# Last inverse roots moved off GpSimd, and shorter final waits, at the end of an eight-core encoder layer

## Chip, cores, metric

One Trainium2 chip, all 8 cores, one launch; each core works on its own two prompt streams (8192 rows) and 32 sample rows. The metric is the device time in microseconds (us) of the slowest core. Executions fall into states: in a *slow* one, one die or both are granted a lower TensorE clock and the time is some per cent longer, whatever the kernel.

Engine names in profile lines: PE is TensorE (PEld its weight loads), DVE VectorE, ACT ScalarE, POOL GpSimd, SP SyncE. A `q` behind a name (SPq) means that the sequencer did it: a wait, a DMA issue, a drain. A semaphore is a counter that a finished instruction or a landed DMA raises and that others wait for; a drain is an instruction at which an engine finishes what it has begun before it goes on.

## The reference, cut to what matters

```python
x = x + rms_norm(merged @ w_out, n_post_mix)
h2 = rms_norm(x, n_pre_ffn)
g, up = jnp.split(h2 @ w_ffn_in, 2, axis=-1)
x = x + rms_norm((jax.nn.silu(g) * up) @ w_ffn_out, n_post_ffn)      # the last step of a tile
# rms_norm(x, g): x * rsqrt(mean(x * x) + 1e-6) * g, in float32
```

The kernel takes 16 tiles of 512 rows, one after the other.

## The kernel before

A small recording layer keeps a list of instructions for each engine and works out the waits. At the end it emits the lists inside a block; the block closes with a drain on each engine and a barrier. SyncE alone waits for all DMA semaphores of the program.

```python
def run(eng_name, e, final=False):
    for o in self.ops[eng_name]:
        ...                                   # the op's own waits, the op, its semaphore (cut)
    if final:                                 # SyncE only
        for k in self.dma_keys:               # 91 semaphores
            e.wait_ge(dsem[k], self.dma_count[k])
```

An inverse root is made of two GpSimd operations on 128x1, multiply-add and power:

```python
def rsqrt(P, c, eps, scale=1.0 / D, eng=POOL):
    o, i_ = stt[0:P, c + 1:c + 2], stt[0:P, c:c + 1]
    ts(eng, o, i_, float(scale), float(eps), ALU.mult, ALU.add, SK(c), SK(c + 1))
    tt(POOL, o, o, negh[0:P, 0:1], ALU.pow, SK(c + 1) + ["negh"], SK(c + 1))   # negh = -0.5
```

In the last tile, row blocks 0 to 2 (128 rows each) go through `PostNorm`: Square with accumulation on ScalarE, `rsqrt`, a multiply and an add on VectorE, a 512 KB store from SyncE. The last row block comes in two halves of 512 columns, so that the first is squared while TensorE makes the second:

```python
def last_rows(n):
    ...
    act(hst[:, n, 0:512], ps[:, b, :], AF.Square, ..., accum_out=stt[:, lc + n:lc + n + 1])
    tt(DVE, lt[:, n, :], ps[:, b, :], gS[:, 3, cs], ALU.mult, ...)
    o = stt[:, lc + 2 + n:lc + 3 + n]
    ts(POOL, o, stt[:, lc + n:lc + n + 1], 1.0 / D, stt[:, lc + 2:lc + 3] if n else EPS, ALU.mult, ALU.add, ...)
    if n == 0:
        return
    tt(POOL, o, o, negh[:, 0:1], ALU.pow, ...)
    for k in range(2):
        sttop(xt[:, 3, cs], lt[:, k, :], o, xt[:, 3, cs], ALU.mult, ALU.add, ...)
        m.dma((SP, ACT)[k], uniq("so"), yp[...], xt[:, 3, cs], ...)          # 256 KB each
```

The softmax here doesn't subtract the row's maximum and nothing guards it: scores larger than these inputs give would overflow.

Of the kernel before, what the change touches and what calls it, by code (L numbers as in the profile page):

```python
# [6 lines left out]
F32 = mybir.dt.float32  # L7
# [9 lines left out]
D = 1024  # L17
# [16 lines left out]
class MK:  # L34
    def __init__(self, nc):
        self.nc = nc
        self.ops = {e: [] for e in ENGS}
        self.last_w = {}
        self.readers = {}
        self.known = {e: [-1] * len(ENGS) for e in ENGS}  # L40
        self.known_dma = {e: {} for e in ENGS}
        self.dma_count = {}
        self.dma_keys = []
        self.pending = {e: [] for e in ENGS}
        self.stage = "setup"

# [23 lines left out]
    def _add(self, eng, emit, reads, writes, dma_sem=None):  # L70
        op = Op(eng, emit)
        op.tag = self.stage
        lst = self.ops[eng]
        op.idx = len(lst)
        deps = self._deps(reads, writes, eng)
        if self.pending[eng]:
            deps.extend(self.pending[eng])
            self.pending[eng] = []
        kn = self.known[eng]
        kd = self.known_dma[eng]  # L80
        best = {}
        for t in deps:
            k = (t[0], t[1])
            o = best.get(k)
            if o is None or t[2] > o[2]:
                best[k] = t
        for t in best.values():
            if t[0] == "e":
                _, de, di, dclk = t
                if de == eng and eng in (PE, SP):  # L90
                    continue
                j = EIDX[de]
                if kn[j] >= di:
                    continue
                if de == eng and eng != POOL and dma_sem is None and op.idx - di >= 4:
                    continue
                op.waits.append(("e", de, di))
                self.ops[de][di].need_inc = True
                kn[j] = di
                for jj, v in enumerate(dclk):  # L100
                    if v > kn[jj]:
                        kn[jj] = v
            else:
                _, sk, val = t
                if kd.get(sk, 0) >= val:
                    continue
                assert val == self.dma_count[sk], ("ambiguous DMA semaphore wait", sk, val, self.dma_count[sk])
                op.waits.append(("d", sk, val))
                kd[sk] = val
        if dma_sem is not None:  # L110
            if dma_sem not in self.dma_count:
                self.dma_count[dma_sem] = 0
                self.dma_keys.append(dma_sem)
            self.dma_count[dma_sem] += 16
            op.dma_sem = dma_sem
            op.dma_val = self.dma_count[dma_sem]
            tok = ("d", dma_sem, op.dma_val)
        else:
            clk = list(kn)
            clk[EIDX[eng]] = op.idx  # L120
            tok = ("e", eng, op.idx, tuple(clk))
        for k in writes:
            self.last_w[k] = tok
            self.readers[k] = []
        for k in reads:
            if k not in writes:
                self.readers.setdefault(k, []).append(tok)
        lst.append(op)
        return op
# [21 lines left out]
    def finish(self):  # L151
        nc = self.nc
        with ExitStack() as st:
            esem = {e: st.enter_context(nc.semaphore("s_" + e)) for e in ENGS}
            dsem = {k: st.enter_context(nc.semaphore("d_%d" % i)) for i, k in enumerate(self.dma_keys)}
            semval = {}
            for e in ENGS:
                c = 0
                vals = []
                for o in self.ops[e]:  # L160
                    if o.need_inc:
                        c += 1
                    vals.append(c)
                semval[e] = vals
            block = st.enter_context(nc.Block())

            def run(eng_name, e, final=False):
                for o in self.ops[eng_name]:
                    for w in o.waits:
                        if w[0] == "e":  # L170
                            e.wait_ge(esem[w[1]], semval[w[1]][w[2]])
                        else:
                            e.wait_ge(dsem[w[1]], w[2])
                    ins = o.emit(e)
                    if o.dma_sem is not None:
                        ins.then_inc(dsem[o.dma_sem], 16)
                    elif o.need_inc:
                        ins.then_inc(esem[eng_name], 1)
                if final:
                    for k in self.dma_keys:  # L180
                        e.wait_ge(dsem[k], self.dma_count[k])

            @block.tensor
            def _(e):
                run(PE, e)

            @block.scalar
            def _(e):
                run(ACT, e)

            @block.vector
            def _(e):
                run(DVE, e)

            @block.gpsimd
            def _(e):
                run(POOL, e)

            @block.sync
            def _(e):  # L200
                run(SP, e, final=True)
# [3 lines left out]
def build_program(n_prompt_tiles=16, do_sample=True):  # L205
# [33 lines left out]
    with ExitStack() as st:  # L239
# [27 lines left out]
        es2 = sb("es2", [128, 8], F32)  # L267
        g0T = sb("g0T", [128, 8], F32)
        negh = sb("negh", [128, 4], F32)
        ident = sb("ident", [128, 128], BF16)  # L270
        ones = sb("ones", [128, 128], BF16)
        WmT = sb("WmT", [128, 4, 128], BF16)
# [31 lines left out]
            m.op(PE, lambda e: e.transpose(out=out, in_=in_, identity=idn), reads=reads + ["ident"],  # L304
                 writes=[("ps", TB)])

        def act(out, in_, func, reads, writes, scale=1.0, accum_out=None):
            kw = {} if accum_out is None else {"accum_out": accum_out}
            m.op(ACT, lambda e: e.activation(out=out, in_=in_, func=func, scale=scale, **kw), reads=reads,  # L309
                 writes=writes)  # L310

# [153 lines left out]
        def rsqrt(P, c, eps, scale=1.0 / D, eng=POOL):  # L465
# [2 lines left out]
            ts(eng, o, i_, float(scale), float(eps), ALU.mult, ALU.add, SK(c), SK(c + 1))  # L468
            tt(POOL, o, o, negh[0:P, 0:1], ALU.pow, SK(c + 1) + ["negh"], SK(c + 1))

        def slot_(P, slot):

            if slot < 2:
                return hst[0:P, slot, :], [("hst", slot)]
            return PT[0:P, slot - 2].rearrange("p h n -> p (h n)"), [("PT", slot - 2)]
# [16 lines left out]
            copy(ACT, dst, pTv[:, 0:8 * P].rearrange("p (k t) -> p k t", k=8), B(TB), dk)  # L492

        class PostNorm:
            def __init__(self, P, pair, gi, x, xk, eps_mul=1.0, dst=None):
                self.P, self.pair, self.gi, self.x, self.xk = P, pair, gi, x, xk
                self.eps, self.dst = EPS * eps_mul, dst

            def square(self, junk=None):
                P, b = self.P, self.pair  # L500
                self.t, self.tk, _ = tmp2()
                self.c = stat(2)
                out, ok = junk or (self.t[0:P], self.tk)
                act(out, ps[0:P, b:b + 2, :], AF.Square, B(b, b + 1), ok + SK(self.c),
                    accum_out=stt[0:P, self.c:self.c + 1])
                rsqrt(P, self.c, self.eps)

            def apply(self):
                P, b = self.P, self.pair
# [36 lines left out]
        m.op(POOL, lambda e: e.memset(negh[:], -0.5), writes=["negh"])  # L546
        act(stt[:, 62:63], negh[:, 0:1], AF.Exp, ["negh"], SK(62))
        m.op(POOL, lambda e: e.memset(ones[:], 1.0), writes=["ones"])
        t0_, t0k = tmp1()
        m.op(POOL, lambda e: e.memset(t0_[:, 0:128], 1.0), writes=t0k)  # L550
        affine(t0_[:, 0:128], [[-1, 128]], ALU.is_equal, 0, 1, t0k[0])
# [863 lines left out]
        def ffn(T, N):  # L1415
# [74 lines left out]
            def last_rows(n):  # L1490
# [2 lines left out]
                b, cs = 6 + n, slice(512 * n, 512 * n + 512)  # L1493
                act(hst[:, n, 0:512], ps[:, b, :], AF.Square, B(b), [("hst", n), *SK(lc + n)],
                    accum_out=stt[:, lc + n:lc + n + 1])
                tt(DVE, lt[:, n, :], ps[:, b, :], gS[:, 3, cs], ALU.mult, B(b) + [("gS", 3)], [ltk[n]])
                o = stt[:, lc + 2 + n:lc + 3 + n]
                ts(POOL, o, stt[:, lc + n:lc + n + 1], 1.0 / D, stt[:, lc + 2:lc + 3] if n else EPS, ALU.mult, ALU.add,
                   SK(lc + n) + (SK(lc + 2) if n else []), SK(lc + 2 + n))
                if n == 0:  # L1500
                    return
                tt(POOL, o, o, negh[:, 0:1], ALU.pow, SK(lc + 3) + ["negh"], SK(lc + 3))
                for k in range(2):
                    cs = slice(512 * k, 512 * k + 512)
                    sttop(xt[:, 3, cs], lt[:, k, :], o, xt[:, 3, cs], ALU.mult, ALU.add,
                          [ltk[k]] + SK(lc + 3) + XK(3), [("xt3", k)])
                    m.dma((SP, ACT)[k], uniq("so"), yp[T["seq"], t0:t0 + 128, cs], xt[:, 3, cs], reads=[("xt3", k)])

            for bl in range(4):
# [6 lines left out]
                if bl == 2 and not N:  # L1516
                    last_rows(0)
                before = pn
                pn = PostNorm(128, 2 * bl, 3, xt[:, bl, :], XK(bl), dst=yp[T["seq"], t0:t0 + 128, :])
                pn.square()  # L1520
                if bl and N:
                    before.store(ACT)
# [145 lines left out]
```

## Time and profile before

| | before |
|---|---|
| first three executions | 4629.0, 4013.2, 4354.0 us (median 4354.0) |
| profiled execution, slowest core (6) | 4015.0 us, granted clock 0.998 |
| last matmul ends, core 6 | 4004.53 us |
| from there to the end of the program (the "tail") | 10.50 us on each of the 8 cores |

The page of the profile, with the span, TensorE's busy time and the chain that ended last:

```profile
span 4015.0 us, 60008 instructions; the slowest of 8 cores (4008.7 to 4015.0 us)
PE 3962.1 (99%) x22234; PEld 1893.3 (47%) x22630; DVE 1752.7 (44%) x1725; ACT 1390.4 (35%) x2144; POOL 806.8 (20%) x1028
...
PE 97%; issue 1%; DMA 1%; DVE 0%; ACT 0%; POOL 0%; DVEq 0%; SPq 0%; POOLq 0%; ACTq 0%
```

TensorE bounds the kernel. What the change can touch is the tail after the last matmul. The timeline of the tail (columns: start us, length us, what, and in brackets how long the engine had been idle and who ended that):

```profile
4004.63 0.60 ACT L309 ACTIVATE hst<-ps 128x512 bf16<-128x512 f32 x1 [3.58 <-PE ps L300]
...
4005.12 0.20 ACT L309 ACTIVATION_READ_ACCUMULATOR hst<-ps 128x1 f32 x1
4005.42 0.69 DVE L319 TENSOR_TENSOR tmp<-ps,gS 128x512 f32<-128x512 f32 x1 [0.61 <-ACT hst L309]
4005.50 0.27 POOL L326 TENSOR_SCALAR stt<-stt 128x1 f32<-128x1 f32 x1 [3.41 <-ACT hst L309]
4005.91 0.55 POOL L319 TENSOR_TENSOR stt<-stt,negh 128x1 f32<-128x1 f32 x1
4006.57 1.41 DVE L330 SCALAR_TENSOR_TENSOR xt<-tmp,stt,xt 128x512 f32<-128x512 f32 x2 [0.46 <-POOL stt L319]
4008.06 0.34 ACTq L136 DMA_DIRECT2D yp<-xt  x1
```

The last store is issued at 4008.06, but the span ends at 4015.03. Neither view shows where those 7 us go: the timeline leaves out the sequencers' waits and drains, and the chain, followed to its end, stops at 4007.98 in VectorE's drain. They are found by asking for the source lines that emit them. Columns: engine, operation and count, length in ns (shortest, median, longest), first and last start in us. The final waits of SyncE:

```profile
L181 SPq EVENT_SEMAPHORE  x91: 17/17/17, 4007.8 to 4012.6; - x91
```

And the drains that close the block:

```profile
L153 PEldq DRAIN  x1: 4075/4075/4075, 4000.5 to 4000.5; - x1
L153 POOLq DRAIN  x1: 8919/8919/8919, 4005.9 to 4005.9; - x1
L153 DVEq DRAIN  x1: 1324/1324/1324, 4006.7 to 4006.7; - x1
L153 ACTq DRAIN  x1: 152/152/152, 4008.4 to 4008.4; - x1
L153 SPq DRAIN  x1: 7/7/7, 4012.7 to 4012.7; - x1
```

GpSimd's drain starts at 4005.88, while its last power still runs, and ends at 4014.80: 8.34 us after the power. The 0.23 us after that are the barrier. SyncE's 91 waits, 0.05 us apart, end at 4012.65. The last store, meanwhile, took (issues by queue in the tail, with KB and us from issue to landing):

```profile
yp<-xt SPq DMA_DIRECT2D x1, 512.0 KB, 2.7
yp<-xt SPq DMA_DIRECT2D x1, 256.0 KB, 2.0
yp<-xt ACTq DMA_DIRECT2D x1, 256.0 KB, 2.0
```

so all data had landed at 4010.10, nearly 5 us ahead of the end.

### The profile page before, as it was taken

The page shows a single profiled execution, that of the slowest core. Times are in us where ns is not written, and L with a number is a line of the kernel's source. Part 1 is how long each engine was busy: PE and PEld are TensorE (multiplying, and loading weights), DVE is VectorE, ACT ScalarE, POOL GpSimd, SP SyncE. Part 2 cuts the span into 40 slices and gives each one's busy share as a digit, 9 for nine tenths or more (in the row PEclk, how much of TensorE's full clock was granted, in tenths as well). Part 3 has the DMA queues.
Part 4 walks back from the last instruction along what each step waited for, and adds up shares of the span by engine and source line. Part 5 has one row for each costly group of instructions (what it writes and reads, how often), then busy time and mean ns, then how long its engine had stood idle before and what let it go on. Part 6 is the DMA issues. An engine that isn't in the chain of part 4 may idle for free.

```text
span 4015.0 us, 60008 instructions; the slowest of 8 cores (4008.7 to 4015.0 us)
## 1 busy us (share of the span) xinstructions
PE 3962.1 (99%) x22234; PEld 1893.3 (47%) x22630; DVE 1752.7 (44%) x1725; ACT 1390.4 (35%) x2144; POOL 806.8 (20%) x1028
## 2 busy tenths in 40 slices
PE   8999999999999999999999999999999999999998
PEld 4544445444444444444444444444444444444444
DVE  4616426163361633616345262442615426163352
ACT  5515325153241423314243142522515224152331
POOL 3204123040220302202031120311203012030220
PEclk9999999999999999999999999999999999999999
DMA  9999998885664645537455464654646445464442
GB/s 174 186 186 210 193 200 217 216 236 160 195 202 154 223 153 181 194 138 232 147 192 184 144 211 163 203 168 161 209 148 208 168 171 198 150 219 151 176 145 81
DMA packets 128326, 727.58 MB, mean 181 GB/s; under 512 B 20142, under 2 KB 22666, under 8 KB 58538
## 3 DMA queue, kind: packets, MB, share of 16 engines
q1 hardware_dynamic: 105088, 603.72, 44.3%
q0 software_dynamic: 15856, 95.57, 14.9%
q10 hardware_dynamic: 7098, 24.42, 1.5%
q8 instruction: 188, 3.08, 0.3%
q14 instruction: 96, 0.79, 0.1%
HBM read 749.06 MB, written 70.08 MB: 204 GB/s over the span
## 4 chain that ended last, share of the span: by engine, by line
PE 97%; issue 1%; DMA 1%; DVE 0%; ACT 0%; POOL 0%; DVEq 0%; SPq 0%; POOLq 0%; ACTq 0%
PE ps L300 96%; PE ps L304 1%; DMA gx<-xp 0%; DMA s_rs<-stt 0%; DVE tmp L330 0%; ACT PT L309 0%; DMA aT<-vecs 0%; DVE hT L330 0%; DMA hst<-s_rs 0%; POOL stt L319 0%; DVE big L330 0%; ACT hst L309 0%; ACT big L309 0%; SPq L136 0%; DVE hst L330 0%
## 5 line engine op out<-in xcount | busy, mean ns | idle before, releaser
L300 PE MATMUL ps<-aT,ring 128*128 128x512 bf16 (+1 forms) x6551 | 1446.0, 378 | 9.6 <-ACT aT L309 1.4
L309 ACT ACTIVATE tmp<-ps 128x512 f32<-128x512 f32 (+2 forms) x614 | 463.1, 765 | 1612.9 <-PE ps L300 1611.7
L300 PEld LDWEIGHTS ps<-aT,ring 128*128 128x128 bf16 x6704 | 655.2, 98 | 774.1 <-issue 1.6
L300 PE MATMUL ps<-hT,ring 128*128 128x512 bf16 x4206 | 965.7, 379 | 12.2 <-issue 3.2
L319 DVE TENSOR_TENSOR big<-ps,tmp 128x512 bf16<-128x512 f32 x352 | 243.2, 691 | 972.4 <-PE ps L300 920.3
L300 PEld LDWEIGHTS ps<-hT,ring 128*128 128x128 bf16 x4352 | 414.1, 98 | 485.8 <-issue 19.9
L300 PE MATMUL ps<-ring,big 128*128 128x512 bf16 x2756 | 605.8, 379 | 3.2
L326 POOL TENSOR_SCALAR stt<-stt 128x1 f32<-128x1 f32 (+2 forms) x289 | 139.0, 481 | 2186.0 <-ACT tmp L309 1777.9
L334 DVE RECIPROCAL tmp<-tmp 128x512 f32<-128x512 f32 x129 | 421.9, 3311 | 127.4 <-POOL tmp L319 127.3
L330 DVE SCALAR_TENSOR_TENSOR tmp<-ps,stt,gS 128x1024 f32<-128x1024 f32 x123 | 157.9, 1283 | 700.0 <-POOL stt L319 679.9
L300 PEld LDWEIGHTS ps<-ring,big 128*128 128x128 bf16 x2816 | 275.2, 98 | 332.6 <-issue 1.3
L300 PE MATMUL ps<-ring,hT 128*128 128x512 bf16 (+1 forms) x1518 | 293.2, 344 | 1.1 <-issue 0.2
L309 ACT ACTIVATE big<-ps 128x512 bf16<-128x512 f32 (+1 forms) x389 | 226.0, 596 | 190.3 <-PE ps L300 186.8
L300 PE MATMUL ps<-big,ring 128*128 128x512 bf16 x1021 | 235.4, 379 | 1.3 <-DVE tmp L330 1.1
L300 PE MATMUL ps<-ring,mgT 128*128 128x512 bf16 x1008 | 225.9, 379 | 2.0 <-DVE mgT L319 1.2
L309 ACT ACTIVATE qT<-ps 128x512 bf16<-128x512 f32 (+1 forms) x132 | 80.1, 606 | 412.0 <-PE ps L300 411.7
L300 PEld LDWEIGHTS ps<-ring,hT 128*128 128x128 bf16 x1536 | 148.1, 98 | 124.2 <-issue 1.3
L319 POOL TENSOR_TENSOR stt<-stt,negh 128x1 f32<-128x1 f32 (+1 forms) x292 | 184.4, 632 | 52.6 <-DVE stt L326 8.7
L319 POOL TENSOR_TENSOR aT<-tmp 128x512 bf16<-128x512 f32 x112 | 142.1, 1269 | 257.6 <-DVE tmp L334 253.3
L309 ACT ACTIVATE PT<-ps 128x1024 bf16<-128x1024 f32 (+1 forms) x192 | 180.7, 1018 | 0.3
L330 DVE SCALAR_TENSOR_TENSOR tmp<-big,ps 128x1024 f32<-128x1024 bf16 x128 | 155.5, 1215 | 54.8 <-PE ps L300 54.8
L319 POOL TENSOR_TENSOR xt<-xt,tmp 128x1024 f32<-128x1024 f32 x60 | 141.6, 2360 | 92.2 <-DVE tmp L330 92.2
(164 smaller groups left out, 2289.6 us busy)
## 6 DMA issues: line engine op xcount, KB each, us to landing
ring<-s_wfi SPq DMA_DIRECT2D x145, 1024.0 KB, 5.5
ring<-s_win SPq DMA_DIRECT2D x136, 1024.0 KB, 6.1
ring<-wb POOLq DMA_DIRECT2D x84, 1024.0 KB, 19.0
ring<-s_wfo SPq DMA_DIRECT2D x58, 1024.0 KB, 4.8
xt<-xp SPq DMA_DIRECT2D x63, 512.0 KB, 11.3
ring<-s_wap SPq DMA_DIRECT2D x30, 1024.0 KB, 7.3
ring<-s_wgp SPq DMA_DIRECT2D x29, 1024.0 KB, 7.4
ring<-s_wout SPq DMA_DIRECT2D x29, 1024.0 KB, 8.8
```

Of the source, the lines that this page charges most:

```text
L300: m.op(PE, lambda e: e.matmul(out, lhsT=lhsT, rhs=rhs, start=start, stop=stop, skip_group_check=True), reads=reads, writes=[("ps", bank)])
L304: m.op(PE, lambda e: e.transpose(out=out, in_=in_, identity=idn), reads=reads + ["ident"], writes=[("ps", TB)])
L309: m.op(ACT, lambda e: e.activation(out=out, in_=in_, func=func, scale=scale, **kw), reads=reads, writes=writes)
L319: m.op(eng, lambda e: e.tensor_tensor(out=out, in0=in0, in1=in1, op=op), reads=reads, writes=writes)
L326: m.op(eng, lambda e: e.tensor_scalar(out=out, in0=in0, scalar1=s1, scalar2=s2, op0=op0, op1=op1), reads=reads, writes=writes)
L330: m.op(DVE, lambda e: e.scalar_tensor_tensor(out=out, in0=in0, scalar=scalar, in1=in1, op0=op0, op1=op1), reads=reads, writes=writes)
L334: m.op(DVE, lambda e: e.reciprocal(out=out, in_=in_), reads=reads, writes=writes)
```

## The change

Its intent: GpSimd should have nothing to do in the last feed-forward, so that its closing drain runs under cover of the matmuls; SyncE should wait only for DMAs that nobody has waited for yet, and for the older of those early.

```diff
@@ finish()
+            left = [k for k in self.dma_keys if self.dma_waited.get(k, 0) < self.dma_count[k]]
+            early = [k for k in left if self.dma_stage[k] != self.stage]
...
-                for o in self.ops[eng_name]:
+                for i, o in enumerate(self.ops[eng_name]):
+                    if final and i == len(self.ops[eng_name]) - 6:
+                        for k in early:
+                            e.wait_ge(dsem[k], self.dma_count[k])
...
                 if final:
-                    for k in self.dma_keys:
-                        e.wait_ge(dsem[k], self.dma_count[k])
+                    for k in left:
+                        if k not in early:
+                            e.wait_ge(dsem[k], self.dma_count[k])
@@ roots of row blocks 0 to 2 of the last tile (PostNorm with last=not N)
+        def rsqrt_act(P, c, bias, bk):
+            o = stt[0:P, c + 1:c + 2]
+            act(o, stt[0:P, c:c + 1], AF.Sqrt, SK(c) + bk, SK(c + 1), scale=1.0 / D, bias=bias)
+            recip(o, o, SK(c + 1), SK(c + 1))
...
@@ last_rows (cut): the first half's sum is scaled on VectorE and becomes the bias of the second's Sqrt
+                if n == 0:
+                    tt(DVE, lt[:, n, :], ps[:, b, :], gS[:, 3, cs], ALU.mult, ...)
+                    ts(DVE, stt[:, lc + 3:lc + 4], stt[:, lc:lc + 1], 1.0 / D, EPS, ALU.mult, ALU.add, ...)
+                    return
+                o = stt[:, lc + 2:lc + 3]
+                act(o, stt[:, lc + 1:lc + 2], AF.Sqrt, ..., scale=1.0 / D, bias=stt[:, lc + 3:lc + 4])
                 tt(DVE, lt[:, n, :], ps[:, b, :], gS[:, 3, cs], ALU.mult, ...)
-                ts(POOL, o, ...)
-                tt(POOL, o, o, negh[:, 0:1], ALU.pow, ...)
+                recip(o, o, SK(lc + 2), SK(lc + 2))
```

Also new: a 128x1 tile `epsb` that holds 1e-6, set once at the start.

More of the change, by code (lines that the diff above doesn't have):

```diff
@@ L43, in __init__ @@
         self.dma_keys = []
+        self.dma_waited = {}
+        self.dma_stage = {}
         self.pending = {e: [] for e in ENGS}
@@ L108, in _add @@
                 op.waits.append(("d", sk, val))
+                self.dma_waited[sk] = max(val, self.dma_waited.get(sk, 0))
                 kd[sk] = val
@@ L114, in _add @@
             self.dma_count[dma_sem] += 16
+            self.dma_stage[dma_sem] = self.stage
             op.dma_sem = dma_sem
@@ L269, in build_program @@
         negh = sb("negh", [128, 4], F32)
+        epsb = sb("epsb", [128, 1], F32)
         ident = sb("ident", [128, 128], BF16)
@@ L305, in tp_, with act @@
                  writes=[("ps", TB)])
-        def act(out, in_, func, reads, writes, scale=1.0, accum_out=None):
+        def act(out, in_, func, reads, writes, scale=1.0, accum_out=None, bias=None):
             kw = {} if accum_out is None else {"accum_out": accum_out}
+            if bias is not None:
+                kw["bias"] = bias
             m.op(ACT, lambda e: e.activation(out=out, in_=in_, func=func, scale=scale, **kw), reads=reads,
@@ L494, in build_program, with __init__ @@
         class PostNorm:
-            def __init__(self, P, pair, gi, x, xk, eps_mul=1.0, dst=None):
+            def __init__(self, P, pair, gi, x, xk, eps_mul=1.0, dst=None, last=False):
+                self.last = last
                 self.P, self.pair, self.gi, self.x, self.xk = P, pair, gi, x, xk
@@ L505, in square @@
                     accum_out=stt[0:P, self.c:self.c + 1])
-                rsqrt(P, self.c, self.eps)
+                if self.last:
+                    rsqrt_act(P, self.c, epsb[0:P], ["epsb"])
+                else:
+                    rsqrt(P, self.c, self.eps)
             def apply(self):
@@ L548, in build_program @@
         m.op(POOL, lambda e: e.memset(ones[:], 1.0), writes=["ones"])
+        m.op(POOL, lambda e: e.memset(epsb[:], EPS), writes=["epsb"])
         t0_, t0k = tmp1()
@@ L1495, in last_rows @@
                     accum_out=stt[:, lc + n:lc + n + 1])
-                tt(DVE, lt[:, n, :], ps[:, b, :], gS[:, 3, cs], ALU.mult, B(b) + [("gS", 3)], [ltk[n]])
-                o = stt[:, lc + 2 + n:lc + 3 + n]
-                ts(POOL, o, stt[:, lc + n:lc + n + 1], 1.0 / D, stt[:, lc + 2:lc + 3] if n else EPS, ALU.mult, ALU.add,
-                   SK(lc + n) + (SK(lc + 2) if n else []), SK(lc + 2 + n))
-                if n == 0:
-                    return
-                tt(POOL, o, o, negh[:, 0:1], ALU.pow, SK(lc + 3) + ["negh"], SK(lc + 3))
+                if n == 0:
+                    tt(DVE, lt[:, n, :], ps[:, b, :], gS[:, 3, cs], ALU.mult, B(b) + [("gS", 3)], [ltk[n]])
+                    ts(DVE, stt[:, lc + 3:lc + 4], stt[:, lc:lc + 1], 1.0 / D, EPS, ALU.mult, ALU.add, SK(lc),
+                       SK(lc + 3))
+                    return
+                o = stt[:, lc + 2:lc + 3]
+                act(o, stt[:, lc + 1:lc + 2], AF.Sqrt, SK(lc + 1) + SK(lc + 3), SK(lc + 2), scale=1.0 / D,
+                    bias=stt[:, lc + 3:lc + 4])
+                tt(DVE, lt[:, n, :], ps[:, b, :], gS[:, 3, cs], ALU.mult, B(b) + [("gS", 3)], [ltk[n]])
+                recip(o, o, SK(lc + 2), SK(lc + 2))
                 for k in range(2):
@@ L1505, in last_rows @@
                     sttop(xt[:, 3, cs], lt[:, k, :], o, xt[:, 3, cs], ALU.mult, ALU.add,
-                          [ltk[k]] + SK(lc + 3) + XK(3), [("xt3", k)])
+                          [ltk[k]] + SK(lc + 2) + XK(3), [("xt3", k)])
                     m.dma((SP, ACT)[k], uniq("so"), yp[T["seq"], t0:t0 + 128, cs], xt[:, 3, cs], reads=[("xt3", k)])
@@ L1518, in ffn @@
                 before = pn
-                pn = PostNorm(128, 2 * bl, 3, xt[:, bl, :], XK(bl), dst=yp[T["seq"], t0:t0 + 128, :])
+                pn = PostNorm(128, 2 * bl, 3, xt[:, bl, :], XK(bl), dst=yp[T["seq"], t0:t0 + 128, :], last=not N)
                 pn.square()
```

## The prediction

> **What bounds the kernel.** TensorE. The page gives PE 3962.1 of 4015.0 us (99%), the chain that ended last is 97% PE, and the granted clock is 0.997 to 0.999 on all cores (view of the cores). The change touches none of that. It works on the tail after the last matmul: on core 6 that matmul ends at 4004.54 and the program at 4015.03, so 10.5 us (0.26%) is all that can be won.
>
> **The tail now** (instructions of core 6 in order of time, sequencer included). Two branches run side by side and meet in the closing barrier:
> - GpSimd: its last 128x1 power ends at 4006.47; its closing DRAIN ends at 4014.80, 8.34 us later. On all eight cores that distance is 8.337 to 8.338 us. The barrier takes 0.23 us more. This branch ends last.
> - SyncE: after its last store issue it makes 91 waits, one for every DMA semaphore, 0.05 us each, from 4007.77 to 4012.69. The last store (queue of ScalarE) had landed at 4010.10, so SyncE is 2.5 us late, yet 2.1 us ahead of GpSimd.
>
> **What the change does.** The order of instructions shows:
> 1. GpSimd loses the ten tiny operations of the last feed-forward stage. Its last work becomes the power that now ends at about 3890.8 (timeline), so its drain should be over by about 3900, under cover of matmuls.
> 2. SyncE waits for 10 semaphores in place of 91: five old ones ahead of its second-last-but-one weight load, five (the stores of y) at the end. Only the last wait should block, until the store lands.
> 3. ScalarE gets four 128x1 Sqrt, VectorE four 128x1 reciprocals and one 128x1 tensor_scalar (0.15 us here). A 128x1 activation took 0.20 us; the pointer bias costs more: the Trainium skill ("ScalarE: Activation LUTs", What ACT_TABLE_LOAD costs) says about 93 ns, so I estimate 0.3 us. The same section says a switch of table set needs a load of 1283 ns; the trace agrees (each of 49 loads 1283 ns). Sqrt needs one more, once: Square follows Gelu, Exp and Silu without loads of its own here. It falls in the first row block, whose next squares come 4.7 us later, so it is hidden.
> 4. One more 128x1 memset (0.10 us) at the start, not on a critical wait.
>
> **Last row block.** Before: accumulator read ends 4005.32, two GpSimd operations, first final multiply-add starts 4006.57. After: Sqrt ends at about 4005.7 beside the VectorE product, which ends at 4006.11; reciprocal, wait, multiply-add at about 4006.35. Gain about 0.2 us, estimated. Last landing about 4009.9; last wait, SyncE drain and barrier about 0.3 us more: end about 4010.2.
>
> **Prediction.** 4.8 us (0.12%) shorter: profile about 4010 us, fast runs about 4008.5 us against 4013.2. Cores of one run spread by 6 us, so fast runs should fall in 4003 to 4014. The three times before (4013, 4354, 4629) show slow executions, which the change can't cure; if the number quoted is a median over states, it may lie far higher. The range on record covers fast runs and a mildly slow median. Faster by 2%: 1%; within 2%: 98%; slower by 2%: 1%, fast against fast.
>
> **Right if:** GpSimd's closing drain ends near 3900; about 5 waits stand between SyncE's last issue and its drain; 50 table loads; last matmul to end about 5.7 us in place of 10.5 on every core; the end follows the last landing by 0.3 us.
>
> **Wrong if:** GpSimd's drain is not a fixed time after its last work but hangs on something at the end of the program (then gain near zero); Square reloads tables between Sqrts (1.28 us each in the last block); the last landing is later because stores run together.

## More of the kernel before

One more thing matters later: in the first tiles GpSimd issues the DMAs that load and convert weights (`ring<-wb`), and twice the stores of key and value rows. The trace has 101 GpSimd DMAs, the last of them near 3660 us.

## The result, and the profile after

The first four executions took 4008.74, 4009.75, 4010.68 (fast) and 4211.51 us (slow), median 4010.2. All ratios here are the mean time of one kernel's fast runs over that of the other's fast runs of the same rounds, so not quite the ratio of medians. It was 0.9992 (95% interval 0.9969 to 1.0014), against only two fast runs of before (4013.2 and 4012.5): 3.1 us between the means.

The trace decides more finely than the time, as the tail hardly varies from core to core. "us after the last matmul" is counted from its end as the profiler models it (4004.53 on core 6 before, 4001.60 on core 4 after, the slowest cores of their runs):

| us after the last matmul | before | after |
|---|---|---|
| accumulator read of the last Square ends | 0.79 | 0.78 |
| first of the two final multiply-adds starts | 2.04 | 1.75 |
| last store issued | 3.53 | 3.24 |
| last store landed | 5.57 | 5.28 |
| SyncE reaches its drain | 8.16 | 5.35 |
| GpSimd's drain ends | 10.27 | 106 us before it |
| end of the program | 10.50 | 5.57 |

On the eight cores after, the end comes 5.57 to 5.62 us after the last matmul, 5.82 on one. It follows the last landing by 0.29 us everywhere (4.7 to 4.9 us before). The tail is 4.9 us shorter. The rest of the 7.8 us between the two profiled spans is only where the last matmul fell on the slowest core.

The page after:

```profile
span 4007.2 us, 59922 instructions; the slowest of 8 cores (4003.2 to 4007.2 us)
PE 3962.4 (99%) x22234; PEld 1892.4 (47%) x22630; DVE 1753.8 (44%) x1730; ACT 1392.3 (35%) x2149; POOL 804.1 (20%) x1020
```

TensorE's busy time is as before; GpSimd has 8 instructions fewer (9 gone, one memset new). The timeline of the tail:

```profile
4001.69 0.60 ACT L323 ACTIVATE hst<-ps 128x512 bf16<-128x512 f32 x1 [3.19 <-PE ps L312]
4002.19 0.19 ACT L323 ACTIVATION_READ_ACCUMULATOR hst<-ps 128x1 f32 x1
4002.48 0.69 DVE L333 TENSOR_TENSOR tmp<-ps,gS 128x512 f32<-128x512 f32 x1 [1.00 <-ACT hst L323]
4002.53 0.29 ACT L323 ACTIVATE stt<-stt 128x1 f32<-128x1 f32 x1
4003.09 0.15 DVE L348 RECIPROCAL stt<-stt 128x1 f32<-128x1 f32 x1
4003.35 1.41 DVE L344 SCALAR_TENSOR_TENSOR xt<-tmp,stt,xt 128x512 f32<-128x512 f32 x2
4004.84 0.34 ACTq L140 DMA_DIRECT2D yp<-xt  x1
```

The Sqrt is hidden beside VectorE's product, so only reciprocal and multiply-adds follow it. The final waits:

```profile
L192 SPq EVENT_SEMAPHORE  x5: 17/17/17, 4004.5 to 4006.9; - x5
```

Five waits, the last of which ends with the landing. The drains:

```profile
L157 POOLq DRAIN  x1: 9701/9701/9701, 3885.9 to 3885.9; - x1
...
L157 SPq DRAIN  x1: 7/7/7, 4007.0 to 4007.0; - x1
```

GpSimd's drain again ends 8.34 us after its last power, but that is at 3895.5, with more than 100 us of matmuls to come. Table loads (group of the lines view: count, busy us, mean ns, idle time before and who ended it; the first line is from before, the others from after):

```profile
L309 ACT ACT_TABLE_LOAD x49 | 62.9, 1283 | 68.7 <-PE ps L300 51.3 <-POOL stt L326 13.3 <-issue 3.7
L323 ACT ACT_TABLE_LOAD x50 | 64.2, 1283 | 68.2 <-PE ps L312 51.3 <-POOL stt L340 12.4 <-issue 4.0
L323 ACT ACTIVATE stt<-stt,epsb 128x1 f32<-128x1 f32 x3 | 0.9, 294 | 0.2
```

One load more than before, in row block 0, where its 1.28 us are hidden. Square needs none between the Sqrts.

### The profile page after: what moved, and what is told of

It reads as the page before. It is cut to its first block, busy times and chain, and to the rows that moved or that the text cites. A ratio compares the mean times of both kernels' runs of the same rounds, so it can differ in the third digit from the quotient of the medians.

```text
span 4007.2 us, 59922 instructions; the slowest of 8 cores (4003.2 to 4007.2 us)
## 1 busy us (share of the span) xinstructions
PE 3962.4 (99%) x22234; PEld 1892.4 (47%) x22630; DVE 1753.8 (44%) x1730; ACT 1392.3 (35%) x2149; POOL 804.1 (20%) x1020
## 3 DMA queue, kind: packets, MB, share of 16 engines
q8 instruction: 188, 3.08, 0.3%
## 4 chain that ended last, share of the span: by engine, by line
PE 96%; DMA 1%; issue 1%; DVE 1%; ACT 0%; POOL 0%; SPq 0%; DVEq 0%; ACTq 0%; POOLq 0%
PE ps L312 95%; DMA s_rs<-stt 1%; PE ps L316 1%; DVE tmp L344 0%; DVE hT L344 0%; DMA hst<-s_rs 0%; DMA xt<-xp 0%; ACT PT L323 0%; POOL stt L333 0%; ACT hst L323 0%; SPq L140 0%; ACT big L323 0%; DVE mgT L333 0%; DVE big L344 0%; DVE hst L344 0%
```

## The experiments

Nine kernels were run, all of them correct. Times and tails of the timed ones in one table; the two first columns of times are means of fast runs of the same rounds on the same chip, in us, with their number:

| kernel | this | before | gain in time | gain, mean of 8 cores | last matmul to end, 8 cores |
|---|---|---|---|---|---|
| after_again | 4008.8 (3) | 4013.7 (7) | 4.9 | 4.5 | 5.58 to 5.88 |
| roots_only | 4011.6 (3) | 4013.7 (7) | 2.1 | 2.5 | 8.09 |
| waits_only | 4013.3 (3) | 4013.7 (7) | 0.4 | 0.0 | 10.50 |
| drain_early | 4011.4 (5) | 4015.2 (5) | 3.9 | 4.4 | 5.85 to 6.12 |
| waits_moved | 4011.1 (3) | 4015.2 (5) | 4.1 | 4.1 | 6.52 to 7.09 |
| store_split | 4010.6 (5) | 4015.2 (5) | 4.6 | 4.8 | 5.76 to 6.02 |
| waits_fewer | 4011.5 (3) | 4016.5 (4) | 5.0 | 5.3 | 5.57 to 5.72 |

The stated 95% intervals of the ratios are about 0.2% wide to each side, so no gain in the time of the slowest core is clear of zero by itself. The mean span of the eight cores, for the same fast runs, is steadier: fast runs of one kernel scatter in it by at most 2.3 us, and in every row but waits_only each run of the changed kernel lies below each run of before. The tails repeat on eight cores; the times of the slowest core agree with them within about 1 us, the means of the cores within about 0.4 us. drain_law was also timed, once (4020.2 us, fast), but its added DMAs make that no measure of the tail.

### after_again

No edit; the changed kernel once more, to size the gain.

> The changed kernel again, to size the gain among fast runs. Theory (the tail after the last matmul is all that changed): last matmul to end 5.6 us on every core in place of 10.5, fast runs 4.9 us (0.12%) shorter, ratio about 0.9988. Rival (something outside the tail moved too, as the 3 us between the first fast runs suggests): a tail of 5.6 us but a gain in time well off 4.9 us, and a last matmul that ends later than before on the mean of the eight cores.

Ratio 0.999 (0.997 to 1.001): 4.9 us between the means, 5.6 to 5.9 us of tail. The theory holds; the 3 us of the first comparison fits scatter between few runs. As to the rival: the mean span of the eight cores is 4004.8 to 4005.7 us in the fast runs here and 4008.7 to 4010.7 in those of before, 4.5 us apart. Less the mean tails (5.7 and 10.5), the last matmul ends at about 3999.5 and 3999.1 us, a difference within the scatter, so nothing outside the tail is seen to have moved. The cores above 5.7 are those whose last store took 2.2 to 2.3 us to land in place of 2.04; before, such a delay was hidden under the drain.

### roots_only

```diff
-                    if final and i == len(self.ops[eng_name]) - 6: ...      # early waits gone
-                    for k in left:
-                        if k not in early:
-                            e.wait_ge(dsem[k], self.dma_count[k])
+                    for k in self.dma_keys:                                 # all 91, as before
+                        e.wait_ge(dsem[k], self.dma_count[k])
```

> The new inverse roots with the old 91 final waits. Theory (two branches run side by side and the later one counts): GpSimd's closing drain is over near 3895, and SyncE's 91 waits of 0.05 us become the branch that ends last: 2.95 us from the last matmul to the first wait, 4.9 us of waits, 0.2 us of barrier: last matmul to end about 8.1 us, gain 2.4 us. Rival (the roots alone made the gain, the waits were already hidden): 5.6 us, gain 4.9 us.

The tail was 8.09 us on all eight cores, as the theory had it. Final waits of this kernel (slowest core, span 4011.8; the trace that was kept is of another execution, span 4013.6, with the same counts and the same tail):

```profile
L188 SPq EVENT_SEMAPHORE  x91: 17/17/17, 4006.6 to 4011.5; - x91
```

and two of its drains:

```profile
L157 POOLq DRAIN  x1: 9699/9699/9699, 3888.1 to 3888.1; - x1
...
L157 SPq DRAIN  x1: 7/7/7, 4011.5 to 4011.5; - x1
```

With GpSimd out of the way, the 91 waits end last, and the program ends 2.5 to 2.8 us after the last landing. The roots alone give 2.4 us of tail.

### waits_only

```diff
-                pn = PostNorm(..., last=not N)
+                pn = PostNorm(..., last=False)          # rsqrt on GpSimd again
 ... last_rows as in the kernel before
```

> The old inverse roots on GpSimd with the new final waits. Theory: GpSimd's closing drain still ends 8.34 us after its last power, so last matmul to end stays 10.5 us and the gain is 0 us, though SyncE reaches its own drain about 4.9 us after the last matmul now. Rival (SyncE's 2.5 us of late waits were on the path): about 8 us, gain 2.5 us.

The tail was 10.50 us on all eight cores. On the slowest core (span 4013.0):

```profile
L157 POOLq DRAIN  x1: 8917/8917/8917, 4003.8 to 4003.8; - x1
...
L157 SPq DRAIN  x1: 7/7/7, 4008.1 to 4008.1; - x1
```

SyncE is done at 4008.1 and stands in the barrier until GpSimd's drain ends at 4012.7. So the waits alone gave 0 us of tail, the roots alone 2.4, both 4.9. Two branches that end in one barrier don't add: the later one counts. A test of the waits alone would have dismissed them.

### drains

What does GpSimd do in 8.34 us? Its drain at the very start of the program took only 0.18 us. This is the kernel *before* with drains added:

```diff
+        m.op(POOL, lambda e: e.drain())                                  # set-up
 ...
         def ffn(T, N):
+            for _ in range({1: 1, 4: 1, 8: 1, 12: 2}.get(T["i"], 0)):
+                m.op(POOL, lambda e: e.drain())
```

> The kernel before with explicit GpSimd drains: one in the set-up ahead of any DMA of GpSimd, one each at the start of the feed-forward of tiles 1, 4 and 8, two in a row at tile 12. Theory A (every drain of GpSimd costs 8.3 us after its last work, whatever stands before it): all about 8.3 us, the set-up's too. B (only the first drain after work of another kind is long, as if code had to be fetched): the first one long, the later ones and the closing one 0.2 us, last matmul to end about 8.3 us, since SyncE's waits then end last. C (long once GpSimd has issued DMAs): set-up's 0.2 us as the 0.18 us of the drain at the program's start, all later ones 8.3 us, last matmul to end 10.5 us. The second of the pair at tile 12 tells if a drain with no work before it costs too.

Its three timed executions were slow, so no time is used; the profile shown has clocks of 0.998 and 0.999 on all cores. The added drains on core 4, of tiles 1, 4, 8 and 12 (the one in the set-up took 0.27 us):

```profile
L1419 POOLq DRAIN  x1: 20915/20915/20915, 452.1 to 452.1; - x1
...
L1419 POOLq DRAIN  x1: 4014/4014/4014, 1184.1 to 1184.1; - x1
...
L1419 POOLq DRAIN  x1: 817/817/817, 2167.4 to 2167.4; - x1
...
L1419 POOLq DRAIN  x2: 47/353/659, 3150.3 to 3151.0; - x2
```

```profile
L153 POOLq DRAIN  x1: 829/829/829, 3997.9 to 3997.9; - x1
```

The line just above is the closing drain of the same core. At tiles 4, 8 and 12 and at the end the drain is entered while the last power still runs (about 0.58 us of the figure). Counted from the end of that power, tile 8's took 0.24 us, tile 12's first 0.08 us, and the closing one 0.25 us instead of 8.34; the tail fell to 8.37 us, where SyncE's 91 waits end it. Theories A (always 8.3 us) and C (always long after the first DMA) fall. B (only the first is long) doesn't fit either: tile 1's drain and tile 4's are both long (both with DMAs in flight, so drain_law settles this better). What does fit is a debt that each drain pays off: 101 GpSimd DMAs had been issued by the drain of 8.34 us, 2 by those of 0.24, none by that of 0.08. Tiles 1 and 4 also had DMAs in flight: on each core, tile 4's drain ended 1.477 us after the last of them landed (1.476 to 1.477), so a drain waits for landings too. How the wait and the debt combine isn't settled.

### drain_law

The new theory, tested with known numbers of DMAs (memory to memory, unused by the result) on the kernel after:

```diff
+            if T["i"] in (6, 8, 10, 12, 14):
+                m.op(POOL, lambda e: e.drain())
+            for n0, n, wide in {6: [(0, 20, 8)], 8: [(20, 20, D)], 10: [(40, 60, 8)]}.get(T["i"], []):
+                for k in range(n0, n0 + n):
+                    m.dma(POOL, "law%d" % n0, s_law[k, :, 0:wide], xp[0, 0:128, 0:wide])
```

> What GpSimd's drain is made of. The kernel after, with a drain of GpSimd at the start of the feed-forward of tiles 6, 8, 10, 12 and 14, and GpSimd DMAs between them (20 of 4 KB, then 20 of 512 KB, then 60 of 4 KB, from memory to memory), all landed long before the next drain. Theory fitted to the earlier runs: 0.08 us after the last work plus 0.082 us for each DMA that GpSimd issued since its last drain (101 DMAs: 8.34; 2: 0.24; none: 0.08), whatever its size. So tile 8 (20 and the 2 of the key and value rows) 1.9 us, tile 10 (20) 1.7 us, tile 12 (60) 5.0 us, tile 14 (none) 0.1 us, the closing one (2) 0.24 us. Rival by bytes (95.6 MB gave 8.26 us): tile 8 0.1 us, tile 10 1.0 us, tile 12 0.1 us. Rival (a fixed 8.3 us after any large batch): 8.3 us or nothing.

The drains of tiles 8, 10 and 12 on core 4:

```profile
L1444 POOLq DRAIN  x1: 2287/2287/2287, 2168.3 to 2168.3; - x1
...
L1444 POOLq DRAIN  x1: 2287/2287/2287, 2666.1 to 2666.1; - x1
...
L1444 POOLq DRAIN  x1: 5549/5549/5549, 3157.5 to 3157.5; - x1
```

From the end of the last power that is 1.707, 1.707 and 4.97 us, the same on every core looked at within 0.002 us: (1.707 - 0.08) / 20 = 0.0814 and (4.97 - 0.08) / 60 = 0.0815 us for each DMA, and (8.338 - 0.08) / 101 = 0.0818 in the kernel before. DMAs of 4 KB and of 512 KB count alike, so the rival by bytes falls. Three expectations missed in detail, all from one oversight: the two key and value stores are issued just in front of the drains of tiles 6 and 14, not behind them. So tile 8 had 20 to pay for, not 22; tile 14's drain waited for two in flight (3.5 us, ending 0.12 us after the later landing on core 4); and the closing drain, with none left, took 0.083 us in place of 0.24.

### drain_early

If so, one drain at a time when nobody needs GpSimd should free the old roots too. (In the sum of the expectation, read: landing about 5.6 us after the last matmul, with the slower roots counted in, plus 0.29.) From `waits_only`:

```diff
         def ffn(T, N):
+            if not N:                                   # the last tile
+                m.op(POOL, lambda e: e.drain())
```

> Old inverse roots on GpSimd, new final waits, and one explicit drain of GpSimd at the start of the last feed-forward, some 110 us before the end. Theory (the drain retires GpSimd's DMAs, once): that drain takes 8.3 us after the last work where nobody needs GpSimd, the closing one 0.08 us, so the last landing ends the program: last matmul to end 4.94 to land plus 0.29, times the 0.62 us in which the roots stay slower counted in: about 5.9 us, gain 4.6 us, nearly the whole of the change without moving one root. Rival (the closing drain costs 8.3 us after any work of GpSimd near the end): 10.5 us, gain 0.

The added drain on core 4, the slowest (span 4010.0), then the closing ones of the same core:

```profile
L1443 POOLq DRAIN  x1: 9697/9697/9697, 3889.6 to 3889.6; - x1
```

```profile
L157 POOLq DRAIN  x1: 653/653/653, 4005.5 to 4005.5; - x1
...
L157 SPq DRAIN  x1: 7/7/7, 4009.8 to 4009.8; - x1
```

The closing drain ends 0.07 us after the last power, and the end follows the landing by 0.29 us. The tail is 5.85 to 6.12 us, so one added instruction and the new waits give 4.4 to 4.65 of the 4.9 us with the roots left on GpSimd. The rest (about 0.3 us) is what Sqrt and reciprocal save.

### waits_moved

```diff
-            left = [k for k in self.dma_keys if self.dma_waited.get(k, 0) < self.dma_count[k]]
+            left = list(self.dma_keys)           # 74 of them early, 17 at the end
```

> The kernel after with none of the 91 waits dropped: those for semaphores last used in an earlier stage (74) stand ahead of the second-last-but-one weight load, the other 17 at the end. Theory (a wait costs 0.05 us of SyncE and only those after the last issue can count, and of those only what exceeds the 2.35 us of landing): 17 waits take 0.9 us, hidden; last matmul to end 5.6 us as after, gain 4.9 us. Rival (each dropped wait was worth its 0.05 us): about 4.3 us longer than after.

A miss: the tail was 6.52 to 7.09 us, 0.9 to 1.5 us more than the theory said (5.6), and far from the rival (4.3 us more: 9.9). The 17 waits were not the delay:

```profile
L192 SPq EVENT_SEMAPHORE  x17: 17/17/17, 4006.1 to 4009.4; - x17
```

The end still follows the last landing by 0.29 us. The landing itself came late (slowest core, issues of the last stores):

```profile
yp<-xt SPq DMA_DIRECT2D x1, 256.0 KB, 2.1
yp<-xt ACTq DMA_DIRECT2D x1, 256.0 KB, 3.0
```

On all eight cores the last store took 2.98 to 3.56 us. The DMA packets of the traces show what is new. Packets on core 7 from the issue of the last store on, grouped by queue, with starts and ends in ns after the issue (in brackets the same core of the kernel after):

```
queue 1  (SyncE's store)    128 packets of 2 KB   first start 115   last end 1044
queue 10 (ScalarE's store)  128 packets of 2 KB   first start 819   last end 2572   (after: 828 to 1725)
queue 14 (instructions)       1 packet of 8 KB    start 1382        end 1809        (after: none)
```

A block of instructions is fetched in the middle of the store. Such a fetch appears near the end on all eight cores here, always with 3 or 4 SyncE instructions to go, and in the kernel before with one to go, when everything has landed; in the kernel after there is none later than about 3900 us. That it is SyncE's is inferred from its instruction count: the trace has 1497 SyncE instructions both here and before, 1416 after.

### waits_fewer

The same 17 final waits, but 40 of the 74 early ones dropped:

```diff
+            covered = [k for k in self.dma_keys if self.dma_waited.get(k, 0) >= self.dma_count[k]
+                       and self.dma_stage[k] != self.stage]
-            left = list(self.dma_keys)
+            left = [k for k in self.dma_keys if k not in covered[:40]]
```

> Why moving the waits cost 1 us that the theory did not foresee: there the last store landed 3.0 to 3.6 us after its issue on all cores in place of 2.04, and on the core whose DMA packets were traced an 8 KB packet of the instruction queue started within that store, when SyncE had four instructions left; in the kernel after no such packet comes at the end. This is the moved-waits kernel with 40 of its 74 early waits dropped and the same 17 final waits. Theory (SyncE's programme is long enough there that its instruction fetch falls into the last store): 40 instructions fewer, no fetch near the end, the store lands in 2.04 us again, last matmul to end 5.6 us. Rival (17 final waits, or waits ahead of the weight load, delay the store): 6.5 to 7.1 us as with the moved waits.

The fetch is gone (the last is near 3900 us on all cores), and the last store:

```profile
yp<-xt ACTq DMA_DIRECT2D x1, 256.0 KB, 2.1
```

It took 2.03 to 2.06 us on seven cores and 2.19 on one, and the tail was 5.57 to 5.72 us. So 17 final waits are indeed free, under the landing; what cost 1 us was the 40 extra waits in SyncE's program (1457 instructions here), though those run some 65 us before the store. That fetch and delay come together and go together is shown; how one 8 KB packet holds up the store by more than its own 0.43 us is not.

### store_split

An attempt at a version that beats the kernel after: the last 256 KB as two stores of 128 KB.

```diff
-                    m.dma((SP, ACT)[k], uniq("so"), yp[...], xt[:, 3, cs], reads=[("xt3", k)])
+                    for q, c0 in ((SP, 0),) if k == 0 else ((ACT, 0), (SP, 256)):
+                        cs = slice(512 * k + c0, 512 * k + (512 if k == 0 else c0 + 256))
+                        m.dma(q, uniq("so"), yp[...], xt[:, 3, cs], reads=[("xt3", k)])
```

> The kernel after with the last 256 KB store in two of 128 KB, one from ScalarE's queue and one from SyncE's. A 512 KB store landed 2.65 us after issue and a 256 KB one 2.04 us, so I estimate 1.75 us for 128 KB: last matmul to end 5.3 us, 0.3 us less than after, too little to see in time. Rival (the landing time is a fixed cost by then, or the two issues disturb each other): 5.6 us or more.

A miss: 5.76 to 6.02 us, 0.2 to 0.4 us worse. The two small stores on the slowest core:

```profile
yp<-xt SPq DMA_DIRECT2D x1, 128.0 KB, 1.9
yp<-xt ACTq DMA_DIRECT2D x1, 128.0 KB, 2.2
```

Both queues issued within 0.01 us of each other; ScalarE's first packet started 1132 ns after its issue (869 on this core in the kernel after), and its store landed after 2.2 us, though it was half the size. This fits the second half of the rival, that the two issues disturb each other; but the packets shrank too, from 2 to 1 KB, and no run separates the two. Another 0.05 us is the end itself, which follows the landing by 0.34 us here. (The edit also moves the early waits by one place, since SyncE has one operation more; cut above.) No version beat the kernel after.

## Why the prediction was right or wrong

Right, with what was measured:

- TensorE bounds the kernel and isn't touched: busy 3962.1 us before, 3962.4 after.
- Two branches, GpSimd's drain ahead of SyncE's waits, and neither part alone enough: 10.50 (waits only), 8.09 (roots only), 5.6 us (both).
- "4.8 us (0.12%) shorter", fast against fast: the tail lost 4.9 us, the fast means of the repeat differ by 4.9 us (0.12%), the means over all cores by 4.5. The first set alone gave 3.1 us (0.08%). The fast runs of both sets fell at 4008.0 to 4010.7 us, inside the text's "4003 to 4014".
- GpSimd's drain "over by about 3900": 3895.5. Five waits after the last issue: 5. 50 table loads: 50. "Last matmul to end about 5.7 us": 5.57 to 5.62 on seven cores, 5.82 on one. The end 0.3 us after the landing: 0.29.
- Sqrt at 0.3 us: 0.294. "Gain about 0.2 us" for the roots: 0.29 (the first multiply-add starts 1.75 us after the last matmul, not 2.04).

Wrong:

- The step that failed is the last one, under "Prediction": the step from the tail to the time. The text forecast "fast runs about 4008.5 us against 4013.2". But the time before that was quoted is 4354.0, a median of three in which two runs were slow (4629.0 and 4354.0 itself). A fast-state number of 4008.5 beside it reads as a gain of 7.9%; the runs show 0.08% in the first set and 0.12% in the repeat, fast against fast. "The range on record covers fast runs and a mildly slow median" made one range out of two quantities, which says nothing about an effect of 4.8 us. Why such medians can't be set against each other, the runs show: the kernel after had medians of 4010.2 and 4470.1 us in two sets, the kernel before 4354.0, 4015.2, 4117.5 and 4018.9, depending on how many slow runs fell in. The sound form was the ratio among fast runs, 0.9988; applied to the quoted median it gives 4354.0 x 0.9988 = 4349 us.
- The drain as a "fixed time after its last work" had the right size for the wrong reason. It is 0.08 us plus 0.082 us for each of the 101 DMAs that GpSimd had issued since its last drain (drain_law). The sum didn't depend on it, but the cure does: one early drain gives the same gain but for 0.3 us.
- GpSimd lost nine operations, not "ten".

Open: what GpSimd does in the 0.082 us for each DMA, how a drain with DMAs in flight adds up, and why the fetched block delays the store by more than its own length.

## What to carry to other kernels

The end of a program is a barrier of branches, so list every engine's last wait and drain, find the later branch, and test parts together as well as alone: here one part was worth nothing without the other. GpSimd, when it has issued many DMAs, can owe its closing drain microseconds (8.3 us for 101; SyncE, which issued more than 700 here, drained in 7 ns); let it drain early, or give it its last work early. Choose a point with none of its DMAs in flight: tile 1's added drain held GpSimd for 20.9 us.

## What the Trainium skill lacked or had wrong

- *VectorE: DVE Perf Modes*, "The DRAIN you can't avoid", tells two kinds of drain apart, the flush after each VectorE operation and the runtime's boilerplate drains of about 12 ns. It has nothing on the drains that close a program's own block, which aren't of that length: 7 ns (SyncE), 0.15 (ScalarE), 1.3 (VectorE), 4.1 (TensorE) and 8.9 us (GpSimd) before; each includes the work still running on its engine.
- *Perfetto Trace Analysis*, "DMA Instruction — SWDGE (GPSIMD)", follows a GpSimd DMA to its last semaphore and has nothing on what it leaves to the next drain: 0.082 us for each DMA, whatever its size (20 of 4 KB or of 512 KB: 1.707 us both), and a drain with DMAs in flight ended only after their landing (by 1.477 us at tile 4).
- *ScalarE: Activation LUTs*, "What ACT_TABLE_LOAD costs", was right on the load (1283 ns) and on a pointer bias (about 93 ns: 294 ns here against 203 for a 128x1 activation without one). The drain of about 1380 ns that it adds to each switch isn't seen at this one: in row block 0 the load started at 3988.64 us, 0.08 us after the instruction before it ended, and the Sqrt behind it at 3989.93.
- *Runtime: NRT & Kernel Launch*, "Instruction fetch mechanics", says that engines fetch by their own DMA queues, in blocks of 16 KB, mostly hidden. Queue 8 here does carry 16 KB a packet (3.08 MB in 188), queue 14 carries 8 KB (0.78 MB in 95), and one such fetch came with a last store about 1 us late (waits_moved).
- No page states the cost of a wait for a semaphore long satisfied: 0.05 us of SyncE each, 4.9 us for 91.
